# Norms of queries applied as per-partition scalars in two attentions of a two-layer encoder, and other PSUM banks for the first projections

## The chip, the core and the metric

The kernel runs on one core of a Trainium2 chip. A core has four compute engines that run at the same time, each with its own queue of instructions. TensorE (PE in the profile) multiplies matrices: it loads a stationary block of 128x128 weights (the rows "PEld") and streams the other operand past it. VectorE (DVE), ScalarE (ACT) and GpSimd (POOL) work elementwise or along rows. SyncE (SP) issues DMAs. Each works through its queue in order here, and waits on semaphores where an instruction needs what another engine has not finished. Matmul results land in PSUM, which this kernel cuts into eight banks of 128 partitions by 512 fp32 values; everything else lies in SBUF.

The metric is device time in microseconds (us). The span is the time from the first to the last instruction of one profiled execution; the time of that execution is a little longer.

## The reference, cut to what matters

The model is an encoder of two layers on 512 positions of width 1024. What the change touches is the mixer's grouped-query attention (GQA: eight query heads of width 64, two key and value heads), the attention over 256 memory tokens, and the final norm:

```python
def rms_norm(x, g):
    y = x * lax.rsqrt(jnp.mean(x * x, axis=-1, keepdims=True) + EPS)
    return y * g
...
    g_q = apply_axial_rope(rms_norm(g_q.reshape(b, s, GQA_Q_HEADS, HEAD_DIM), q_norm), cos, sin)
    g_k = apply_axial_rope(rms_norm(g_k.reshape(b, s, GQA_KV_HEADS, HEAD_DIM), k_norm), cos, sin)
...
    sc = jnp.einsum('bqkgd,bskd->bkgqs', qi, k) * scale      # GQA, one block of 128 queries
    p = jax.nn.softmax(sc, axis=-1)
    return jnp.einsum('bkgqs,bskd->bqkgd', p, v)
...
    x = x + hybrid_mixer(rms_norm(x, norm_mix[l]), ...)      # NA heads and GQA heads, then w_out
    x = x + memory_cross_attention(rms_norm(x, norm_mem_q[l]), rms_norm(mem, norm_mem_kv[l]), ...)
    x = x + conv_ffn(rms_norm(x, norm_ffn[l]), ...)
return rms_norm(x, norm_final)
```

The norm of a query head is one number per position and head. It scales a whole row of scores, so it may be applied before the scores, or in the exponential of the softmax: exp(r * s - r * max s), with r the norm of that row. The neighbourhood attention (NA) takes the other eight heads; the conv-FFN multiplies by 1024x5632 and 2816x1024.

## The kernel before, in words

**Number format and layout.** All matmuls are fp32 accurate: each operand is split in a high part (rounded, fp32r) and a low part (the rest), and most products are made as three matmuls, hi x hi, hi x lo, lo x hi (`mm3`, `gemm_T`, recorded at line 77). Activations are kept transposed: features on partitions, 512 positions along the row. Weights stream in by DMA as `raw`; ACT casts them to `hi` (L265) and POOL subtracts to get `lo` (L266); four buffers of each are in flight.

**Stages of a layer.** (1) projections of NA, in pairs of heads, and NA attention; (2) the projections of GQA; (3) GQA attention, 16 units of two heads and 128 queries; (4) the output projection's NA half, the memory's keys and values, the output projection's GQA half, closing the residual row by row (`close`, L425 to L444) into the next norm; (5) memory attention, 8 units of one head and 256 queries; (6) the FFN; (7) after the second layer the final norm and output.

**What orders the work.** PE and SP run in the order of the program text. ACT, DVE and POOL are ordered by a list scheduler of the build, in which `behind(n)` shifts an instruction's priority. The text's order comes from three helpers. `weave` runs the stages of an attention (scores, normalise, transpose, values) for staggered units. A `Filler` (`attn_fill`, `ms`) holds a list of generators, such as projections, and hands out pieces of them between the weave's steps; NA_FILL and GQA_FILL say how many. `late(n, f)` puts off a piece of work by n ticks, so that its PE instructions stand behind others while another engine prepares its operands. A moved tick moves everything that stands behind it.

**PSUM.** Three pools: `ps_mm` with four banks (projections, outputs), `ps_s` with two (scores), `ps_t` with two (transposes, sums over partitions). A bank is reused in turn; a matmul into it waits until the last reader of its former content is done.

**A GQA projection** (`gqa_project`, `gqa_rope`, L809 to L883) comes in the order k, q0, q1, v, q2, q3; each holds two heads. 48 matmuls of 128x512 fill a bank. ACT reads it twice (L840 times the gain, L841 squared) and DVE once (L842, times the cosine table). One tick later `swap` moves rows by four DMAs, and four matmuls of the squares against the constant `pairs` give the sums of squares per head and position; DVE makes the variance (L852, L855). After another tick `rotate` lets POOL take the power -1/2 (L862), copy it to whole rows (L863), and finish the rotation (L864, L865). Two ticks later `norm` turns these rows by four matmuls against the identity into a bank, L868 to L871; these are the records `mm<-ident,t`. One tick later DVE multiplies (L875) and the product is split: `split_q` (ACT copies L682, DVE subtractions L684) or `split_k` (L664, L668).

**A GQA unit** (`gqa_scores`, L888 to L904): two matmuls for each of two heads give 128x512 scores; DVE takes the negated maximum (L900), ACT the exponential with the maximum as bias and the sum accumulated (L902). `gqa_normalise` takes the reciprocal (L908) and POOL multiplies (L479). `gqa_transpose_p` follows on PE (L64), ACT (L472) and DVE (L473).

**A memory unit** (`mem_scores`, L1069 to L1084): DVE takes the negated maxima of two query blocks at once (L1076) and multiplies them by the norm `mq.rstd` (L1077), ACT takes two exponentials with that bias and the norm as scale (L1081); `normalise` (L479) is a DVE tensor_scalar whose factor is read per partition from SBUF:

```python
def normalise(e, sums, col, eng=DVE):
    eng.tensor_scalar(e, e, sums[:, col : col + 1], 1.0, op0=ALU.mult, op1=ALU.mult)
```

**The first projections** of layer 0 (`project_first`) take q0, k0 and q1 of NA interleaved as their inputs arrive, each into a bank of `ps_mm`; in layer 1 `project_qk` does the same one after the other. `split_qk` reads these banks (L650, L664 to L684). `attn_fill.step(N_FIRST ...)` (L1029) sets how many pieces run before the first scores; the pieces behind them are NA's value blocks `project_v`, each a 128x256 product in a bank of `ps_mm`.

**The final norm** (L1232 to L1253): each row is scaled by its gain `gfin` on ACT (L1241), after its square has been added up.

Of the kernel before, what the change touches and what calls it, by code (L numbers as in the profile page):

```python
# [13 lines left out]
ALU = mybir.AluOpType  # L14
# [38 lines left out]
W_BEHIND, N_RAW, N_W, AHEAD, AHEAD_HELD, N_WARM, N_LATE, N_FIRST = 45, 2, 4, 2, 5, 8, 4, 3  # L53
# [120 lines left out]
def encoder_kernel(ctx: ExitStack, tc: tile.TileContext, t: dict, out: bass.AP):  # L174
# [357 lines left out]
    mem_rep = cpool.tile([P, MEMN], F32, name="mem_rep")  # L532

# [55 lines left out]
    for l in range(DEPTH):  # L589
# [11 lines left out]
        def project_first():  # L601

            w, pms = {}, {}
            for u, k0, k1 in ((0, 0, 2), (1, 0, 2), (0, 2, 4), (1, 2, 4), (2, 0, 4), (0, 4, 6),
                              (1, 4, 6), (2, 4, 6), (0, 6, 8), (1, 6, 8), (2, 6, 8)):
                if u not in w:
                    w[u], pms[u] = get_w(NA_ORDER[u]), ps_mm()
# [23 lines left out]
        def project_qk(n, p):  # L631
            w = get_w((n, p))
            pm = ps_mm()
            gemm_T(pm, w, xg, range(0, 4), 0, KC - 1)
            yield
            gemm_T(pm, w, xg, range(4, 8), 0, KC - 1)
            if (n, p) == ("q", 0):
                mix.stat()
                held.append(pm)
            elif (n, p) == ("k", 0):  # L640
                mix.spread()
                split_qk("q", 0, held.pop())
                split_qk("k", 0, pm)
            else:
                split_qk(n, p, pm)
            yield
# [188 lines left out]
        def gqa_rope(g, pm):  # L835

            gain = qkg[:, l, 0:1] if g != "k" else qkg[:, l, 1:2]
# [6 lines left out]
            def swap():  # L844
# [3 lines left out]
                pv = ps_t()  # L848
# [9 lines left out]
            def rotate(xr, v):  # L858
                r = small(2 * NB)
                rows = tmp()  # L860
                with behind(-40):
                    POOL.tensor_tensor(r, v, mhalf[:, : 2 * NB], op=ALU.pow)  # L862
                    POOL.tensor_copy(rows.rearrange("p (b d) -> p b d", d=HD), r.unsqueeze(2).to_broadcast([P, 2 * NB, HD]))  # L863
                POOL.tensor_mul(xr, xr, gtab[0][:, 1])  # L864
                POOL.tensor_add(xr, cc, xr)  # L865
                late(2, lambda: norm(xr, rows))

            def norm(xr, rows):  # L868
# [3 lines left out]
                late(1, lambda: split(xr, pr))  # L872

            def split(xr, pr):
                DVE.tensor_mul(pr, xr, pr)  # L875
                if g == "k":
                    gk.extend(rtile((2, S)) for _ in range(2))
                    split_k(pr, gk, False)
                else:
                    gq[g] = rtile((2, S))  # L880
                    split_q(pr, gq[g])
# [6 lines left out]
        def gqa_scores(u):  # L888
# [9 lines left out]
            for j in range(2):  # L898
                c = slice(j, j + 1)
                DVE.tensor_reduce(nmx[:, c], sc[j], axis=AX.X, op=ALU.max, negate=True)  # L900
                e = tmp()
                ACT.activation(e, sc[j], AF.Exp, bias=nmx[:, c], accum_out=sums[:, c])  # L902
# [126 lines left out]
        attn_fill.step(N_FIRST if l == 0 else N_FIRST + 5)  # L1029
# [39 lines left out]
        def mem_scores(u):  # L1069
# [7 lines left out]
            DVE.tensor_mul(nmx, nmx, mq.rstd[:, 2 * bp : 2 * bp + 2])  # L1077
# [154 lines left out]
        def down_last(g):  # L1232
# [5 lines left out]
            def scale(half, m):  # L1238
                xc = xT[m][:, 256 * half : 256 * half + 256]
                with behind(20):  # L1240
                    ACT.activation(xc, xc, AF.Copy, scale=gfin[:, m : m + 1])  # L1241
# [135 lines left out]
```

## Time and profile before

| | us |
|---|---|
| runs: median of 3 (lowest, highest) | 1391.63 (1390.44, 1395.34) |
| profiled execution, its own time | 1393.77 |
| its span | 1392.0 |
| PE busy | 1354.7 |
| PE weight loads busy | 1157.8 |
| DVE busy | 834.8 |
| ACT busy | 711.8 |
| POOL busy | 719.3 |
| mean granted TensorE clock (share of full speed) | 0.994 |

The profile gives the busy time of each engine, groups of instructions by line, engine and operation (name of output <- names of inputs, partitions x elements; "x80 | 12.2, 303 | 0.0" is a count, the sum in us, the mean in ns, and the idle time ahead of them), the waits of an engine by what ended them, windows of time with the busy time of each engine, and the timeline. "L900" is line 900 of the kernel before; a line inside a helper is shared by all that call it. PE's matmuls overlap, so a group's sum on PE is more than the time it takes; differences of start times give that.

In the layers' order the stages lie at: start and NA 0 to 97 us, GQA projections 97 to 160, the rest of GQA to about 278, memory attention to 320, FFN to 704, and in layer 1 in the same order from 704 to the end, with GQA projections around 800 to 851, memory attention around 960 to 1000 and the final norm at the end.

### The profile page before, as it was taken

The numbers are of one execution on the slowest core, as the hardware profiler recorded it, in microseconds if no ns is written. First come the engines' busy times: TensorE is split into PE (matmuls) and PEld (weight loads), VectorE is DVE, ScalarE is ACT, GpSimd is POOL, SyncE is SP. The second block draws the span as 40 slices with busy tenths as digits, with TensorE's granted clock in tenths as the row PEclk, the third lists the DMA queues.
The fourth block names the chain that finished last, engine by engine and source line by source line (L and its number), as shares of the span: only waits on it lengthen the run. The fifth ranks groups of instructions, "written<-read, shape, count | busy, mean of one in ns | idle before, by whom it ended". The sixth has DMA issues, their size and how long they took to land.

```text
span 1392.0 us, 19198 instructions
## 1 busy us (share of the span) xinstructions
PE 1354.7 (97%) x7072; PEld 1157.8 (83%) x7072; DVE 834.8 (60%) x1430; ACT 711.8 (51%) x1321; POOL 719.3 (52%) x537
## 2 busy tenths in 40 slices
PE   8999899999999999999999989999999999999997
PEld 7897789877888888888888978998788888888897
DVE  6666766364787177357446556754638843871873
ACT  6676577655443134234557656766554422432453
POOL 2458776635444444444645677756264444444441
PEclk9999999999999999999999999999999999999999
DMA  7653312422333333333356523223133333333331
GB/s 214 185 145 96 87 46 66 116 63 61 98 100 103 94 91 97 101 94 94 105 147 169 139 72 95 65 71 112 40 98 97 101 91 97 98 93 106 90 93 61
DMA packets 218205, 138.83 MB, mean 100 GB/s; under 512 B 6016, under 2 KB 211072, under 8 KB 218112
## 3 DMA queue, kind: packets, MB, share of 16 engines
q1 hardware_dynamic: 217968, 137.60, 34.6%
q8 instruction: 56, 0.92, 0.3%
q14 instruction: 37, 0.30, 0.1%
q10 hardware_dynamic: 144, 0.00, 0.0%
HBM read 125.00 MB, written 2.10 MB: 91 GB/s over the span
## 4 chain that ended last, share of the span: by engine, by line
PE 89%; DVE 4%; ACT 4%; issue 1%; DMA 1%; POOL 0%; DVEq 0%; ACTq 0%; SPq 0%
PE mm L77 82%; PE sc L77 4%; PE tr L64 3%; PE tr L77 1%; ACT hi L265 1%; DVE r L473 1%; DMA raw<-in_w_in 1%; ACT t L745 1%; DVE s L900 1%; DVE s L1077 1%; DVE xg L473 0%; DVE t L842 0%; ACT t L841 0%; ACT t L840 0%; ACT xg L438 0%
## 5 line engine op out<-in xcount | busy, mean ns | idle before, releaser
L266 POOL TENSOR_TENSOR lo<-raw,hi 128x1024 fp32r<-128x1024 f32 (+2 forms) x268 | 499.0, 1874 | 496.9 <-ACT hi L265 468.9
L77 PE MATMUL mm<-xg,hi 128*128 128x512 f32 x1984 | 617.7, 393 | 3.1 <-DVE t L842 2.9
L77 PEld LDWEIGHTS mm<-xg,hi 128*128 128x128 f32 x1984 | 370.4, 189 | 78.9 <-DVE t L842 3.3
L265 ACT CAST hi<-raw 128x512 fp32r<-128x512 f32 (+2 forms) x276 | 224.6, 837 | 346.7 <-PE mm L77 292.9
L77 PE MATMUL mm<-xg,lo 128*128 128x512 f32 x992 | 387.3, 391 | 0.0
L77 PE MATMUL mm<-r,hi 128*128 128x512 f32 (+1 forms) x1144 | 331.6, 374 | 2.3 <-ACT t L444 2.2
L77 PEld LDWEIGHTS mm<-r,hi 128*128 128x128 f32 x1144 | 207.3, 188 | 39.7 <-ACT t L444 3.1
L1201 DVE SCALAR_TENSOR_TENSOR t<-t,par,t 128x7 f32<-128x7 f32 (+1 forms) x352 | 201.9, 641 | 34.0 <-ACT t L1194 34.0
L77 PEld LDWEIGHTS mm<-xg,lo 128*128 128x128 f32 x992 | 187.1, 189 | 39.6
L77 PE MATMUL mm<-r,lo 128*128 128x512 f32 (+1 forms) x572 | 213.4, 373 | 0.0
L77 PEld LDWEIGHTS mm<-r,lo 128*128 128x128 f32 x572 | 108.0, 189 | 19.0
L1186 DVE TENSOR_TENSOR t<-mm,rep 128x512 f32<-128x512 f32 x88 | 60.1, 687 | 78.2 <-PE mm L77 62.1
L479 POOL TENSOR_SCALAR t<-t,s 128x512 f32<-128x512 f32 (+1 forms) x112 | 66.3, 608 | 75.4 <-DVE s L908 35.4
L1203 ACT ACTIVATE t<-t 128x512 f32<-128x512 f32 x44 | 27.8, 633 | 134.8 <-DVE t L1201 134.7
L1207 DVE TENSOR_TENSOR r<-t,r 128x512 fp32r<-128x512 f32 x44 | 90.5, 2056 | 7.4 <-ACT r L1206 4.3
L1230 DVE TENSOR_TENSOR xT<-xT,mm 128x512 f32<-128x512 f32 x32 | 21.9, 685 | 106.8 <-PE mm L77 106.8
L64 PE MATMUL tr<-ident,t 128*128 128x128 f32 x456 | 63.2, 275 | 13.3 <-DVE r L473 3.8
L77 PE MATMUL sc<-r,r 128*128 128x256 f32 (+1 forms) x352 | 72.6, 338 | 3.5 <-DVE r L473 2.5
L64 PEld LDWEIGHTS tr<-ident,t 128*128 128x128 f32 x456 | 52.4, 141 | 22.9 <-issue 9.7
L1194 ACT ACTIVATE t<-t,par 128x512 f32<-128x512 f32 x88 | 66.8, 806 | 3.2 <-DVE t L1186 3.2
L77 PE MATMUL mm<-r,r 128*128 128x256 f32 (+1 forms) x428 | 61.8, 297 | 0.0
L77 PEld LDWEIGHTS sc<-r,r 128*128 128x128 f32 x352 | 52.1, 192 | 8.3 <-DVE r L473 3.0
(145 smaller groups left out, 1554.1 us busy)
## 6 DMA issues: line engine op xcount, KB each, us to landing
raw<-in_w_up SPq DMA_DIRECT2D x88, 512.0 KB, 3.9
raw<-in_w_in SPq DMA_DIRECT2D x33, 512.0 KB, 4.5
raw<-in_w_down SPq DMA_DIRECT2D x32, 448.0 KB, 3.9
raw<-in_w_mem_kv SPq DMA_DIRECT2D x16, 512.0 KB, 4.0
raw<-in_w_down SPq DMA_DIRECT2D x16, 512.0 KB, 4.2
r<-in_bias SPq DMA_DIRECT2D x16, 384.0 KB, 5.8
r<-r SPq DMA_DIRECT2D x22, 256.0 KB, 5.2
raw<-in_w_out SPq DMA_DIRECT2D x8, 512.0 KB, 3.8
```

What stands on the lines that cost most here:

```text
L64: return lambda *a, **k: self.tc.keep_in_program_order(op(*a, **k))
L77: return self.tc.keep_in_program_order(self.engine.matmul(out, lhsT, rhs, **k))
L265: act.copy(hi[:, k], raw[:, k])
L266: (POOL if eng[0] == "P" else DVE).tensor_sub(lo[:, k], raw[:, k], f(hi)[:, k])
L473: DVE.tensor_sub(lo, ps, f(hi))
L479: eng.tensor_scalar(e, e, sums[:, col : col + 1], 1.0, op0=ALU.mult, op1=ALU.mult)
L1186: DVE.tensor_mul(u, us[side], ffn.rep)
L1194: ACT.activation(cc, u, AF.Identity, bias=par[:, l, CB + ch : CB + ch + 1], scale=w[1])
L1201: DVE.scalar_tensor_tensor(cc[:, dst], u[:, src], wi, cc[:, dst], op0=ALU.mult, op1=ALU.add)
L1203: ACT.activation(cs[0], cs[0], AF.Silu)
L1207: DVE.tensor_sub(acts[j][1], cs[0], f(acts[j][0]))
L1230: DVE.tensor_add(xT[m], xT[m], pm)
```

## The change

For q the head norm stays a column per head and position: `rotate` writes it into one of four tiles `qr`, and `gqa_scores` multiplies the negated maximum by it with `normalise` and gives it to the exponential as its scale. The copy to rows, the four matmuls against the identity and the multiplication are left for k alone; q is split from the rotated tile `xr` in SBUF, one tick after the rotation. The sums of pairs go into a bank of `ps_mm` instead of `ps_t`. In the memory attention the product of two columns becomes two calls of `normalise`. The first two projections of each layer use the score banks. N_FIRST goes from 3 to 4 (one piece more ahead of the first scores in layer 0; in layer 1 the sum stays 8). The final gain is multiplied on DVE instead of ACT.

```diff
--- before.py
+++ after.py
@@ -50,7 +50,7 @@
 MEM_FILL = [1, 1, 2, 2, 1, 3, 1, 3, 1, 3, 1]
 N_ROWS = 3
 MEM_STEPS = [0, 0, 1, 0, 1, 1, 1, 1, 1, 1, 1] + [0] * 9
-W_BEHIND, N_RAW, N_W, AHEAD, AHEAD_HELD, N_WARM, N_LATE, N_FIRST = 45, 2, 4, 2, 5, 8, 4, 3
+W_BEHIND, N_RAW, N_W, AHEAD, AHEAD_HELD, N_WARM, N_LATE, N_FIRST = 45, 2, 4, 2, 5, 8, 4, 4
 
 
 class InOrder:
@@ -530,6 +530,7 @@
 
     mem_rstd = cpool.tile([P, MB], F32, name="mem_rstd")
     mem_rep = cpool.tile([P, MEMN], F32, name="mem_rep")
+    qr = [cpool.tile([P, 2 * NB], F32, name=f"qr{i}") for i in range(4)]
 
     def mem_stat():
         raw = load_mem()
@@ -604,7 +605,7 @@
             for u, k0, k1 in ((0, 0, 2), (1, 0, 2), (0, 2, 4), (1, 2, 4), (2, 0, 4), (0, 4, 6),
                               (1, 4, 6), (2, 4, 6), (0, 6, 8), (1, 6, 8), (2, 6, 8)):
                 if u not in w:
-                    w[u], pms[u] = get_w(NA_ORDER[u]), ps_mm()
+                    w[u], pms[u] = get_w(NA_ORDER[u]), ps_s() if u < 2 else ps_mm()
                 if (u, k0) == (0, 0):
 
                     for k in range(2):
@@ -630,7 +631,7 @@
 
         def project_qk(n, p):
             w = get_w((n, p))
-            pm = ps_mm()
+            pm = ps_mm() if p else ps_s()
             gemm_T(pm, w, xg, range(0, 4), 0, KC - 1)
             yield
             gemm_T(pm, w, xg, range(4, 8), 0, KC - 1)
@@ -834,6 +835,7 @@
 
         def gqa_rope(g, pm):
 
+
             gain = qkg[:, l, 0:1] if g != "k" else qkg[:, l, 1:2]
             xs, sq, cc = tmp(), tmp(), tmp()
             with behind(-20):
@@ -845,7 +847,7 @@
                 xr = tmp()
                 for i in range(4):
                     SP.dma_start(xr[32 * i : 32 * i + 32], xs[32 * (i ^ 1) : 32 * (i ^ 1) + 32])
-                pv = ps_t()
+                pv = ps_mm()
                 for b in range(NB):
                     PE.matmul(pv[:, 2 * b : 2 * b + 2], sq[:, b * P : (b + 1) * P], pairs, start=True, stop=True)
                 v = small(2 * NB)
@@ -856,29 +858,38 @@
                 late(1, lambda: rotate(xr, v))
 
             def rotate(xr, v):
-                r = small(2 * NB)
-                rows = tmp()
+                r = small(2 * NB) if g == "k" else qr[g]
                 with behind(-40):
                     POOL.tensor_tensor(r, v, mhalf[:, : 2 * NB], op=ALU.pow)
-                    POOL.tensor_copy(rows.rearrange("p (b d) -> p b d", d=HD), r.unsqueeze(2).to_broadcast([P, 2 * NB, HD]))
+                if g == "k":
+                    rows = tmp()
+                    with behind(-40):
+                        POOL.tensor_copy(rows.rearrange("p (b d) -> p b d", d=HD), r.unsqueeze(2).to_broadcast([P, 2 * NB, HD]))
                 POOL.tensor_mul(xr, xr, gtab[0][:, 1])
                 POOL.tensor_add(xr, cc, xr)
-                late(2, lambda: norm(xr, rows))
+                if g == "k":
+                    late(2, lambda: norm(xr, rows))
+                else:
+                    late(1, lambda: split(xr))
 
             def norm(xr, rows):
                 pr = ps_mm()
                 for b in range(NB):
                     PE.matmul(pr[:, b * P : (b + 1) * P], rows[:, b * P : (b + 1) * P], ident, start=True, stop=True)
-                late(1, lambda: split(xr, pr))
-
-            def split(xr, pr):
-                DVE.tensor_mul(pr, xr, pr)
+
+                def apply():
+                    DVE.tensor_mul(pr, xr, pr)
+                    split(pr)
+
+                late(1, apply)
+
+            def split(src):
                 if g == "k":
                     gk.extend(rtile((2, S)) for _ in range(2))
-                    split_k(pr, gk, False)
+                    split_k(src, gk, False)
                 else:
                     gq[g] = rtile((2, S))
-                    split_q(pr, gq[g])
+                    split_q(src, gq[g])
 
             late(1, swap)
 
@@ -897,9 +908,11 @@
             es = []
             for j in range(2):
                 c = slice(j, j + 1)
+                r = 2 * b + j
                 DVE.tensor_reduce(nmx[:, c], sc[j], axis=AX.X, op=ALU.max, negate=True)
+                normalise(nmx[:, c], qr[i], r)
                 e = tmp()
-                ACT.activation(e, sc[j], AF.Exp, bias=nmx[:, c], accum_out=sums[:, c])
+                ACT.activation(e, sc[j], AF.Exp, bias=nmx[:, c], scale=qr[i][:, r : r + 1], accum_out=sums[:, c])
                 es.append(e)
             ga[u] = es, sums
 
@@ -1026,7 +1039,7 @@
             out_na(), memory_keys(), memory_values(0),
             close_rows(2, PartsView(parts, 4), lambda k: whole[k], lambda: nns.append(Norm(G_MQ, l)) or nns[0],
                        memory_values(1)))
-        attn_fill.step(N_FIRST if l == 0 else N_FIRST + 5)
+        attn_fill.step(N_FIRST if l == 0 else N_FIRST + 4)
 
         def na_quanta(s):
             if s == 3:
@@ -1074,7 +1087,8 @@
                 mm3(sc[:, i, :], *(v[:, qs] for v in mqs[h]), *memk[h], True, True)
             nmx, sums = small(2), small(2)
             DVE.tensor_reduce(nmx, sc, axis=AX.X, op=ALU.max, negate=True)
-            DVE.tensor_mul(nmx, nmx, mq.rstd[:, 2 * bp : 2 * bp + 2])
+            for i in range(2):
+                normalise(nmx[:, i : i + 1], mq.rstd, 2 * bp + i)
             e = tmp((2, 256))
             for i in range(2):
                 b = 2 * bp + i
@@ -1237,8 +1251,7 @@
 
             def scale(half, m):
                 xc = xT[m][:, 256 * half : 256 * half + 256]
-                with behind(20):
-                    ACT.activation(xc, xc, AF.Copy, scale=gfin[:, m : m + 1])
+                DVE.tensor_scalar(xc, xc, gfin[:, m : m + 1], 1.0, op0=ALU.mult, op1=ALU.mult)
 
             def finish(norm):
                 norm.spread()
```

## The prediction, made before the changed kernel ran

> **What bounds the kernel now.** I read the page first (busy times, the chain that ended last), then a table of busy times by stage, then PE's waits in the stages that the change touches.
>
> ```profile
> PE 1354.7 (97%) x7072; PEld 1157.8 (83%) x7072; DVE 834.8 (60%) x1430; ACT 711.8 (51%) x1321; POOL 719.3 (52%) x537
> ...
> PE 89%; DVE 4%; ACT 4%; issue 1%; DMA 1%; POOL 0%; DVEq 0%; ACTq 0%; SPq 0%
> ```
>
> PE is busy for 1354.7 of 1392.0 us; 37 us are all that any better order can win, beside PE work taken out. Work on the other engines counts only where PE waits for it. Where PE is idle:
>
> ```profile
> 118.00:143.00 25.00, 21.66 (x128) 18.61 (x127) 15.89 (x26) 13.99 (x26) 18.34 (x17) 1.00 0.32 85
> 143.00:160.00 17.00, 15.67 (x82) 13.40 (x81) 9.85 (x20) 8.96 (x19) 13.64 (x14) 0.90 0.49 139
> ...
> 190.00:278.00 88.00, 87.03 (x561) 78.82 (x561) 50.34 (x94) 62.28 (x133) 61.19 (x58) 1.00 0.29 82
> 278.00:320.00 42.00, 39.44 (x213) 32.87 (x212) 25.13 (x57) 21.65 (x52) 10.57 (x5) 1.00 0.19 56
> 320.00:704.00 384.00, 382.88 (x1702) 317.04 (x1701) 228.56 (x318) 158.47 (x216) 185.86 (x90) 1.00 0.34 98
> ```
>
> Columns: window, its length, busy us of PE, its weight loads, VectorE (DVE), ScalarE (ACT) and GpSimd (POOL), granted clock, DMA share, GB/s. The feed-forward stretch from 320 has 1.1 us of idle PE and is not touched. The GQA projections (118 to 160) have 4.7 us and a clock below 1, the memory attention (278 to 320) has 2.6. These and the start are the places that decide.
>
> **The change part by part.** *The head norm of q.* PE loses four matmuls for each of eight q's; those for k stay.
>
> ```profile
> 116.66 1.05 PE L77 MATMUL mm<-ident,t 128*128 128x128 f32 x8
> 117.46 0.36 PE L77 MATMUL mm<-r,r 128*128 128x256 f32 x1
> ...
> L863 POOL COPY t<-s 128x512 f32<-128x512 f32 x10 | 6.1, 611 | 0.0
> ...
> L875 DVE TENSOR_TENSOR mm<-t,mm 128x512 f32<-128x512 f32 x10 | 7.0, 696 | 11.8 <-PE mm L77 10.5 <-POOL r L524 0.7 <-issue 0.7
> ```
>
> The eight records of one norm hold PE for 117.46 - 116.66 = 0.80 us. Eight q's give 6.4, and one of them stands in a half-clock stretch, so 0.8 more: -7.2 us. If half of them only stand in front of a wait, it is -3.6. POOL also loses eight copies of 0.61 and DVE eight products of 0.70, which is beside PE's work.
>
> *The first projections.* q0 and k0 take the score banks, so the v blocks find their own banks free, and one block more comes before the first scores.
>
> ```profile
> 34.84 0.35 PE L77 MATMUL mm<-hi,xg 128*128 128x256 f32 x1 [1.51 <-DVE r L684]
> ...
> 38.56 0.39 PE L77 MATMUL sc<-r,r 128*128 128x256 f32 x1 [0.27 <-DVE r L670]
> ```
>
> The block at 34.84 starts 1.51 us early, and with another block in front the scores need not wait: 1.51 + 0.27 is 1.8; the spread across block and scores (one block lasts 2.9 us, 34.84 to 37.77) leaves room for 0.4 more, so -2.2, with 0.4 to 2.5 as its ends. In layer 1 PE waits nowhere here: 0.
>
> *Memory attention.* The product of maxima and norms becomes two per-partition scalar operations.
>
> ```profile
> L1077 DVE TENSOR_TENSOR s<-s,s x16: 140/150/1917, 285.9 to 992.5; 128x2 f32<-128x2 f32 x16
> ...
> 302.64 2.38 POOL L266 TENSOR_TENSOR lo<-raw,hi 128x1024 fp32r<-128x1024 f32 x1 [7.18 <-ACT hi L265]
> 303.13 1.91 DVE L1077 TENSOR_TENSOR s<-s,s 128x2 f32<-128x2 f32 x1
> ...
> PEld sc L77 <- DVE r L473: 1.5, 1, 1.5
> PEld tr L64 <- DVE t L479: 1.2, 1, 1.2
> ```
>
> Of sixteen operations of 0.15 us some last far longer, the longest 1.91 us, while POOL's subtraction of two SBUF tensors runs; DVE is held up behind it, and in the stage the two waits of PE's weight loads above follow, 2.7 us a layer. An extra 0.15 us of DVE per unit eats 0.3 of it: 2.4 per layer, -4.7 in both. If the new form waits for POOL as well it is 0 or +0.3; if all goes, -5.4.
>
> Which it is, these rows say:
>
> ```profile
> L479 DVE TENSOR_SCALAR t<-t,s x32: 343/348/356, 288.9 to 994.5; 128x256 f32<-128x256 f32 x32
> ...
> L855 DVE TENSOR_SCALAR s<-s x10: 165/212/553, 104.1 to 836.2; 128x8 f32<-128x8 f32 x10
> ...
> L1207 DVE TENSOR_TENSOR r<-t,r x44: 680/2414/2474, 365.3 to 1347.9; 128x512 fp32r<-128x512 f32 x44
> ```
>
> The same form on 256 columns (L479, scalar by pointer) never leaves 343 to 356 ns. L855, with constants, once took 0.55. I side with L479, which has the added operation's operands. [...]
>
> *Scores of q.* Every head's maximum gains such an operation (64 of about 0.15 us) between maximum and exponentials; a unit's chain grows by 0.2 to 0.4.
>
> ```profile
> 224.09 0.30 PE L64 MATMUL tr<-ident,t 128*128 128x128 f32 x1 [0.90 <-DVE s L908]
> ```
>
> PE is busy for 87.03 of 88.00 us from 190 to 278, so in most steps the chain is covered. In a step without filler it is not: one such stall of 0.90 per layer now. The changed order has two such steps in layer 0 and one in layer 1: 0.9 + 3 x 0.3 is about +2 (1.5 to 2.5; 0 if the cover holds).
>
> *The split of q and the banks of the pairs' sums.* Losing the norm's three ticks, q is split two or three ticks earlier, from SBUF, and the order of everything behind it shifts. Now PE's weight loads wait thus between 95 and 190 (first four rows; the columns are the sum, the number and the longest), and these durations set such waits:
>
> ```profile
> PEld tr L64 <- issue: 3.1, 3, 2.1
> ...
> PEld tr L77 <- ACT t L841: 1.8, 1, 1.8
> PEld mm L77 <- DVE t L842: 1.6, 1, 1.6
> ...
> PEld tr L77 <- DVE r L473: 0.5, 1, 0.5
> ...
> L840 ACT ACTIVATE t<-mm,qkg 128x512 f32<-128x512 f32 x5 | 3.5, 693 | 0.1
> L841 ACT ACTIVATE t<-mm 128x512 f32<-128x512 f32 x5 | 3.0, 597 | 0.0
> L842 DVE SCALAR_TENSOR_TENSOR t<-mm,qkg,r 128x512 f32<-128x512 f32 x5 | 3.8, 750 | 4.3 <-ACT t L841 4.3
> ...
> L684 DVE TENSOR_TENSOR r<-mm,r 64x512 fp32r<-64x512 f32 x8 | 5.5, 689 | 1.7 <-ACT r L682 1.6
> ...
> L266 POOL TENSOR_TENSOR lo<-raw,hi 128x512 fp32r<-128x512 f32 x16 | 20.5, 1295 | 5.8 <-ACT hi L265 5.8
> L862 POOL TENSOR_TENSOR s<-s,mhalf 128x8 f32<-128x8 f32 x5 | 8.2, 1648 | 3.2 <-DVE s L855 3.1
> L864 POOL TENSOR_TENSOR t<-t,r 128x512 f32<-128x512 f32 x5 | 6.4, 1290 | 3.4 <-DVE r L473 2.7 <-DMA t<-t 0.8
> L865 POOL TENSOR_TENSOR t<-t,t 128x512 f32<-128x512 f32 x5 | 6.4, 1286 | 0.1
> L500 POOL TENSOR_TENSOR r<-t,r 128x512 fp32r<-128x512 f32 x3 | 3.8, 1281 | 2.3 <-PE mm L77 1.6 <-ACT r L499 0.7
> ```
>
> Layer 0 loses 2.1 + 1.8 + 1.6 + 0.5 = 6.0 us in the GQA projections, and layer 1, whose stretch from 800 to 851 has 6.3 us of idle PE (first row of the next fence), about as much. Followed through the changed order, PE meets in layer 0:
> - q1's projection, which waits for the bank of q0's (0.69 + 0.60 on ACT, then 0.75 on DVE, behind one weight cast): 2.5;
> - q2's projection, now whole in one piece, which waits for v's bank, whose reader is queued behind q0's two subtractions (2 x 0.69): 0.7 to 4, taken as 2;
> - q3's pairs straight behind its projection, so both ACT reads bare and their hand-overs, with weight casts between: 2.4;
> - the NA output's first rows, in one piece, which need the last NA pair's low part (L500). On POOL it stands behind a weight split, two rotations and a power: 1.30 + 2 x (1.29 + 1.29) + 1.65 + 1.28 = 9.4, begun 1.3 (both ACT reads) after the projection's end; PE's own work up to there is about 6.8: 3.9.
>
> Sum 10.8 (9.5 to 14.6). Layer 1, in the same way: 3.4 for q0's bank behind two transposes, 2.3 for q1's, 3.0 for the third transpose, and 4.0 for q3's pairs, whose bank is read only after six other DVE operations: 12.5 (10.5 to 15). Beside 6.0 each that is +11.3 (+8 to +17.6). If the orders are looser than that, 0.
>
> *Clock.* Such stalls can cost twice:
>
> ```profile
> 800.00:851.00 51.00, 44.65 (x242) 38.12 (x240) 30.34 (x54) 30.30 (x66) 40.87 (x45) 0.93 0.34 98
> ...
> 150.80:154.00 3.20, 3.20 (x13) 2.87 (x12) 0.32 (x1) 0.00 (x0) 3.20 (x5) 0.51 0.71 191
> ...
> 148.91 0.27 PE L77 MATMUL tr<-pairs,t 128*128 128x2 f32 x1 [1.33 <-ACT t L841]
> ...
> 138.67 0.30 PE L64 MATMUL tr<-ident,t 128*128 128x128 f32 x1 [1.91 <-DVE r L473]
> ```
>
> Soon after the 1.33 at 148.91 PE ran 3.2 us at half clock, which costs 1.6; the 1.91 at 138.67, in the stretch 118 to 143 with its clock of 1.00, was followed by none. I add one such stretch: +1.6 (0 to +4.8). [...]
>
> *Final scale.* Sixteen ACT operations become DVE's.
>
> ```profile
> 1383.70 0.16 DVE L400 TENSOR_SCALAR s<-tr 128x2 f32<-128x2 f32 x1 [1.37 <-PE tr L77]
> ```
>
> The last one, 0.35 us on DVE (L479's row), fits into DVE's 1.37 us of idleness before L400: 0; if it comes later, +0.35.
>
> **Sum.** -7.2 - 2.2 - 4.7 + 2 + 11.3 + 1.6 = +0.8 us. The profiled execution took 1393.77, its span and 1.8 around it, and stands 2.1 above the runs' median of 1391.63; so 1394.6 for such an execution, 1392.4 for the median.
>
> **The rivals.** *A: the stalls at the GQA start don't grow.* For it: freed banks and 0.70 + 0.61 us less DVE and POOL work for each q; against it the queues above. The terms left are -14.1 + 2 = -12.1, with 0 to +4 of new waits: 1379.5 to 1384, about 1381.
> *B: slower, by the subtractions of q's split.* They now have two SBUF inputs, while POOL is busy for 18.34 of 25 us at 118 to 143. L1207 shows that pair at 2.41 instead of 0.69. A collision adds 0.6 (half of a weight split of 1.30) to a DVE queue on which PE waits. Sixteen of them at 0.6 are 9.6; it decides from seven on (4.2 us): about 1402.
> *C: 128x1 operations wait for POOL as L855 once did.* The memory term is 0 instead of -4.7, and the GQA chains lose some 2 more: +7.5, 1399. L479 speaks against it.
> *D: the edit takes matmuls out only ahead of waits*, so that -7.2 is -3.6: +4.4, 1396.
>
> **How the numbers follow.** About 0.3%, 4.2 us, is what a measurement of this kernel can tell from no change. My forecast (1386 to 1398) 0.38, of which 0.12 faster, 0.20 same, 0.06 slower; A 0.27, faster; B 0.18, slower; C 0.09, slower; D 0.08, half same, half slower. That is faster 0.39, same 0.24, slower 0.37. The range reaches from A's end to B's and 2 beyond, 1379 to 1404; the forecast's own is 1386 to 1398.
>
> **What would show it.** mm<-ident,t at 16 records where there are 80; no wait for L684's successor near 34.8; the two memory waits gone and no 128x1 operation above 0.3 us; q's subtractions at 0.69 or longer beside POOL; PE idle for about 10 us between 118 and 160, 4.7 now. The prediction is wrong if that idle time is not larger, if those subtractions are longer than 1.3 us, or if the clock falls more than twice per layer.

## The result: 0.7% slower

The changed kernel takes 1402.71 us (median of 5 runs, 1400.41 to 1404.04) where the kernel before, in its 5 runs, takes 1392.13 (1390.44 to 1395.34): a ratio of 1.0067 with a 95% interval of 1.0047 to 1.0087, or +9.3 us. The profiled execution took 1403.0 us, its span is 1401.2, 9.2 longer than before. Below, a run's difference in us is what its ratio has above or below 1, times 1392.

The page of the changed kernel, its busy times and its chain:

```profile
PE 1355.3 (97%) x7008; PEld 1152.0 (82%) x7008; DVE 845.5 (60%) x1518; ACT 707.8 (51%) x1305; POOL 719.5 (51%) x529
...
PE 85%; DVE 5%; ACT 4%; POOL 2%; DMA 2%; issue 1%; SPq 0%; DVEq 0%; ACTq 0%; POOLq 0%
```

PE has 64 records less, but is busy for 0.6 us more, and idle for 1401.2 - 1355.3 = 45.9 us where it was 37.3. So 8.6 of the 9.2 us are waits. That PE's busy time did not fall by the 6.4 us of the matmuls agrees with the clock: its mean is 0.989 where it was 0.994. What full speed would have saved is 0.011 x 1401 = 15.4 us now and 0.006 x 1392 = 8.4 before, so some 7 us more are lost to reduced speed (about 1 either way, by the rounding of the clock).

The windows of the GQA projections, the GQA attention and the memory attention, and three short stretches (columns as in the prediction's tables):

```profile
118.00:160.00 42.00, 36.38 (x183) 30.25 (x181) 28.98 (x48) 26.70 (x53) 35.71 (x35) 0.92 0.37 102
...
190.00:280.00 90.00, 85.19 (x540) 75.33 (x539) 52.02 (x110) 62.68 (x132) 57.81 (x54) 0.98 0.25 71
282.00:327.00 45.00, 44.66 (x237) 37.13 (x236) 27.34 (x71) 24.79 (x57) 12.72 (x6) 1.00 0.16 48
140.20:143.60 3.40, 3.40 (x18) 3.21 (x18) 2.23 (x5) 1.26 (x3) 3.40 (x4) 0.59 0.40 101
150.80:154.10 3.30, 3.30 (x9) 2.58 (x9) 2.58 (x4) 3.25 (x6) 2.31 (x3) 0.53 0.00 1
256.60:260.00 3.40, 3.40 (x10) 2.60 (x9) 2.05 (x3) 1.53 (x2) 1.97 (x2) 0.54 0.56 167
```

The memory attention lost its idle time (0.3 of 45 us; 2.6 of 42 before). The projections have 5.6 us instead of 4.7, and the GQA attention, which had 1.0 of 88, has 4.8 of 90. From 118 us on, layer 0 has the three slow stretches of the last rows, where before had one. The same stages of layer 1, before and then after:

```profile
800.00:851.00 51.00, 44.65 (x242) 38.12 (x240) 30.34 (x54) 30.30 (x66) 40.87 (x45) 0.93 0.34 98
851.00:966.00 115.00, 114.03 (x715) 102.20 (x714) 65.95 (x122) 79.86 (x173) 77.74 (x77) 1.00 0.26 74
...
802.00:855.00 53.00, 44.34 (x218) 36.26 (x217) 29.87 (x57) 31.68 (x66) 41.17 (x39) 0.90 0.33 97
855.00:975.00 120.00, 114.28 (x703) 99.90 (x702) 67.59 (x147) 79.92 (x170) 77.97 (x79) 1.00 0.24 70
```

There the projections are idle for 8.7 us instead of 6.3, and what follows them, which had 1.0, for 5.7. So in both layers the idle time grew more behind the projections than in them. The timeline of PE names the waits, in layer 0 and then in layer 1:

```profile
139.88 1.07 PE L77 MATMUL mm<-pairs,t 128*128 128x2 f32 x8 [2.07 <-ACT t L843]
...
148.79 0.50 PE L77 MATMUL mm<-r,hi 128*128 128x512 f32 x1 [2.26 <-ACT r L499]
...
150.58 0.50 PE L77 MATMUL mm<-r,hi 128*128 128x512 f32 x1 [1.29 <-POOL r L500]
...
183.47 0.63 PE L64 MATMUL tr<-ident,t 128*128 128x128 f32 x4 [2.91 <-POOL t L479]
...
256.14 0.50 PE L77 MATMUL mm<-r,hi 128*128 128x512 f32 x1 [1.95 <-POOL r L492]
...
825.13 1.08 PE L64 MATMUL tr<-ident,t 128*128 128x128 f32 x4 [4.08 <-DVE r L473]
...
839.02 1.05 PE L77 MATMUL mm<-pairs,t 128*128 128x2 f32 x8 [2.62 <-ACT t L843]
...
944.25 0.50 PE L77 MATMUL mm<-r,hi 128*128 128x512 f32 x1 [1.95 <-POOL r L492]
```

The first three are the pairs of q3 and the NA output's rows; the prediction had these, and in layer 1 the transposes at 825 and the pairs at 839. It did not have the other three: transposes that wait for POOL at 183, and the output projection that waits for the last folded halves (L492) at 256, and the same at 944 in layer 1. Taking the same instruction in both traces as a landmark: the first scores of NA stand 0.5 us later, with a block of 2.9 us more done; the first memory scores of layer 0 4.4 us later (284.17 to 288.56), the last 2.3 later; the last wait for the closing of layer 1's memory attention 6.9 later (1008.61 to 1015.53), and the end 9.2. So each layer loses about 7 us between its first scores and its memory attention, and gets 2.1 back there.

The durations of what was added, by line:

```profile
L479 DVE TENSOR_SCALAR s<-s,qr x64: 194/204/216, 149.4 to 923.2; 128x1 f32<-128x1 f32 x64
L479 DVE TENSOR_SCALAR s<-s,s x32: 201/204/216, 290.3 to 1000.3; 128x1 f32<-128x1 f32 x32
...
L685 DVE TENSOR_TENSOR r<-t,r x16: 684/687/1724, 122.9 to 847.6; 64x512 fp32r<-64x512 f32 x16
...
L915 ACT ACTIVATE t<-sc,s,qr 128x512 f32<-128x512 f32 x64 | 49.4, 777 | 32.9 <-DVE s L479 32.8
...
L1254 DVE TENSOR_SCALAR xT<-xT,gfin x16: 340/347/2001, 1358.5 to 1391.5; 128x256 f32<-128x256 f32 x16
```

None of the 96 operations of 128x1 is over 0.216 us, though 37 of them began while POOL worked on two tensors; q's subtractions reach 1.72, and the exponentials went from 0.693 to 0.777.

### The profile page after: what moved, and what is told of

Read it like the earlier page. It is cut to its first block, busy times and chain, and to the rows that moved or that the text cites. A ratio compares the mean times of both kernels' runs of the same rounds, so it can differ in the third digit from the quotient of the medians.

```text
span 1401.2 us, 19111 instructions
## 1 busy us (share of the span) xinstructions
PE 1355.3 (97%) x7008; PEld 1152.0 (82%) x7008; DVE 845.5 (60%) x1518; ACT 707.8 (51%) x1305; POOL 719.5 (51%) x529
## 4 chain that ended last, share of the span: by engine, by line
PE 85%; DVE 5%; ACT 4%; POOL 2%; DMA 2%; issue 1%; SPq 0%; DVEq 0%; ACTq 0%; POOLq 0%
PE mm L77 77%; PE sc L77 4%; PE tr L64 3%; DMA raw<-in_w_in 1%; ACT hi L265 1%; DVE s L912 1%; PE tr L77 1%; POOL lo L266 1%; DVE xg L473 1%; ACT t L915 1%; SPq L64 0%; POOL t L479 0%; DMA raw<-in_w_down 0%; DMA r<-in_memT 0%; DVE t L455 0%
## 5 line engine op out<-in xcount | busy, mean ns | idle before, releaser
L77 PE MATMUL mm<-xg,hi 128*128 128x512 f32 x1920 | 596.0, 392 | 1.4 <-DVE t L844 1.4
L77 PEld LDWEIGHTS mm<-xg,hi 128*128 128x128 f32 x1920 | 357.9, 189 | 73.5 <-DVE t L844 1.6
L77 PE MATMUL mm<-xg,lo 128*128 128x512 f32 x960 | 374.5, 390 | 0.0
L77 PE MATMUL mm<-r,hi 128*128 128x512 f32 (+1 forms) x1144 | 335.6, 377 | 10.0 <-POOL r L492 3.9
L77 PEld LDWEIGHTS mm<-xg,lo 128*128 128x128 f32 x960 | 180.6, 188 | 38.2
L479 POOL TENSOR_SCALAR t<-t,s 128x512 f32<-128x512 f32 (+1 forms) x112 | 66.2, 607 | 77.7 <-DVE s L921 35.2
L915 ACT ACTIVATE t<-sc,s,qr 128x512 f32<-128x512 f32 x64 | 49.4, 777 | 32.9 <-DVE s L479 32.8
```

The source lines that it names most:

```text
L77: return self.tc.keep_in_program_order(self.engine.matmul(out, lhsT, rhs, **k))
L915: ACT.activation(e, sc[j], AF.Exp, bias=nmx[:, c], scale=qr[i][:, r : r + 1], accum_out=sums[:, c])
```

## The experiments

**One part at a time.** Four kernels carry one part of the change each, on the kernel before.

```diff
# mem_only
-            DVE.tensor_mul(nmx, nmx, mq.rstd[:, 2 * bp : 2 * bp + 2])
+            for i in range(2):
+                normalise(nmx[:, i : i + 1], mq.rstd, 2 * bp + i)
# banks_only: the three lines of project_first, project_qk and N_FIRST (and N_FIRST + 4)
# pairs_only
-                pv = ps_t()
+                pv = ps_mm()
# qnorm_only: rotate, norm, split and gqa_scores as changed, all else as before
```

> Kernel before with only the memory attention's product of maxima and norms as two per-partition scalar operations. Theory 1 (each part acts in its own stage, and the traces of before and after show it there): memory attention shorter by 2.1 us in each layer, nothing elsewhere, so 4.2 us faster (ratio 0.997); the 1.5 us waits of the weight loads of the memory's scores are gone and no 128x1 operation is over 0.3 us. Rival (the stage is bound by PE and the gain in the changed kernel came from what ran before it): below 1.5 us.

> Kernel before with only the first two projections of a layer in the score banks, and one value block more ahead of the first scores in layer 0. Theory 1: 2 to 2.5 us faster, all in layer 0 before 110 us: the wait of 1.51 us at the second value block and of 0.27 at the scores go. Rival (the block that is taken earlier is missing as filler later on): 0 to 1 us faster, with a new wait between 90 and 190 us.

> Kernel before with only the sums of pairs in the projections' banks. Theory 1: within 3 us of before, since the waits for the transposes' banks ahead of the pairs (0.5 us a layer) go and the ring of four banks has one user more. Rival (the projections' banks are scarce): slower by 4 to 12 us, with new waits of projections and outputs for a bank between 97 and 190 and between 800 and 860 us.

> Kernel before with only q's head norm as the exponentials' scale (maxima multiplied, q split from SBUF one tick after the rotation); sums of pairs stay in the transposes' banks. Theory 1 (the loss of the whole change is q's norm, by the order of the work that shifts): slower by 8 to 16 us although PE loses 6.4 us of matmuls. Rival (the sums of pairs in the projections' banks are what costs): faster by 0 to 6 us.

| kernel | ratio to before (95%) | us |
|---|---|---|
| mem_only | 0.9973 (0.9963 to 0.9983) | -3.8 |
| banks_only | 0.9990 (0.9981 to 0.9999) | -1.4 |
| pairs_only | 1.0000 (0.9991 to 1.0008) | 0 |
| qnorm_only | 1.0180 (1.0166 to 1.0194) | +25.1 |

Memory is as theory 1 has it. In its window from 270 to 320 PE's weight loads waited thus before: 1.5 (scores), 1.2 (transposes), 0.9 and 0.4; with the new form, in the same window:

```profile
PEld tr L64 <- issue: 1.1, 2, 0.7
PEld tr L64 <- DVE t L479: 0.5, 1, 0.5
PEld mm L77 <- DVE r L473: 0.2, 1, 0.2
```

The banks are worth less than the stalls that they remove. In the profiled execution PE is idle for 1390.2 - 1355.6 = 34.6 us instead of 37.3, which is theory 1's size, but it is busy for 0.9 us longer, at a mean clock of 0.992 instead of 0.994. Between 90 and 190, where the rival looked for its wait, there is only one of 0.55 us, at 147.26. But with the block taken earlier a longer one comes further on:

```profile
251.34 0.80 PE L77 MATMUL mm<-r,hi 128*128 128x512 f32 x1 [1.95 <-POOL r L492]
```

Before does not wait here. It has 1.4 us of other products (from 249.01) behind the last units' values, which now stand ahead of them, and POOL makes the folded half ahead of its weight splits, where it now stands behind two of them, 2.51 us in all. A slow stretch goes with the wait: the matmul behind it takes 0.80 us, where that at 256.14 in the changed kernel takes 0.50. So the rival's cause is there, beside theory 1's, and the wait at 256 in layer 0 of the changed kernel comes with the banks alone. In layer 1, where the number of pieces ahead of the scores stays 8, banks_only has no such wait. Also, in each of its runs the time is 2.2 us over the span, where it is 1.8 in before's: 0.4 of the gain is lost outside the span, which no run explains. The pairs' bank does nothing alone. q's norm costs more than the whole change does, although it takes matmuls out. Its waits are those of the changed kernel and longer ones; three of the longest in layer 0, from PE's timeline:

```profile
138.94 0.63 PE L64 MATMUL tr<-ident,t 128*128 128x128 f32 x4 [4.09 <-DVE r L473]
...
152.02 1.05 PE L77 MATMUL tr<-pairs,t 128*128 128x2 f32 x8 [2.62 <-ACT t L843]
...
261.56 0.50 PE L77 MATMUL mm<-r,hi 128*128 128x512 f32 x1 [1.95 <-POOL r L492]
```

**Why q's norm costs.** The `Filler` subtracts from what it owes the modelled time of every matmul that is issued in a step, whoever issues it. Without the norm's matmuls (NB, which is 4, at 107 ns each: 428 ns for each q) it hands out pieces earlier, and PE's whole order behind the first q changes. Three kernels separate this from the work itself. The first is q's norm with the missing time still counted and q split at its old tick, so that PE's order is that of before less 32 matmuls; the other two keep PE's order and add one piece of q's new work each.

```diff
# qnorm_counted, against qnorm_only
-                    late(1, lambda: split(xr))
+                    def count():
+                        PE.ns += NB * 107.0
+                        late(1, lambda: split(xr))
+
+                    late(2, count)
# sbuf_split, against before: for q, split from SBUF
+                if g != "k":
+                    DVE.tensor_mul(xr, xr, pr)
+                    pr = xr
+                else:
+                    DVE.tensor_mul(pr, xr, pr)
# max_ops, against before (one_col is a column of ones)
+                normalise(nmx[:, c], one_col, 0)
-                ACT.activation(e, sc[j], AF.Exp, bias=nmx[:, c], accum_out=sums[:, c])
+                ACT.activation(e, sc[j], AF.Exp, bias=nmx[:, c], scale=one_col, accum_out=sums[:, c])
```

> q's head norm as the exponentials' scale, alone as in the run with q's norm only, but the four matmuls that go are still counted (428 ns) when the filler hands out pieces, and q is split at its old tick: PE's order is that of before with 32 matmuls left out. Theory 2 (the 25 us that q's norm cost alone come from the filler: it counts the modelled time of every matmul, so that without the norm's it hands out pieces in another order, and projections come straight behind the work that they wait for): all but 5 us of the 25 go, 1384 to 1396. Rival 2a (the subtractions from SBUF and the longer way from maximum to exponential cost it): it stays at 1408 or more.

> Kernel before, with q's product with its norm written to SBUF instead of PSUM, and q split from there: PE's order is that of before, DVE's sixteen subtractions have two SBUF inputs. Theory 2: under 4 us slower; sixteen subtractions of 0.69 to 1.7 us each, 0.26 us more on average as in the changed kernel's trace, partly beside PE's work. Rival 2a: 8 us or more.

> Kernel before, with every maximum of the grouped-query attention multiplied by a column of ones in a per-partition scalar operation, and that column as the exponential's scale: PE's order is that of before, 64 operations of 0.20 us more on DVE and exponentials of 0.78 instead of 0.69 us. Theory 2: 1 to 4 us slower, in the steps without filler. Rival 2a: 8 us or more.

| kernel | ratio to before (95%) | us |
|---|---|---|
| qnorm_counted | 1.0068 (1.0056 to 1.0081) | +9.5 |
| sbuf_split | 1.0022 (1.0012 to 1.0031) | +3.1 |
| max_ops | 1.0039 (1.0025 to 1.0053) | +5.4 |

The counted time takes 15.6 of the 25.1 us away, so on the kernel before the order is the larger part; but it leaves 9.5, more than theory 2 had, and less than its rival. The two kinds of work, 3.1 and 5.4, were both above or near the upper end of what was expected of them. They add up to 8.5. If they add up in the kernel as well, which no run shows, the 32 matmuls changed the time by about +1 instead of -6.4.

Since PE's order is the same but for the norms, the traces of before and qnorm_counted can be laid side by side, instruction by instruction. The eight norms do go, and save 8.3 us where they stood (0.81 to 0.89 each, and 1.56 for the two in slow stretches). The gain is lost at other places. PE's timeline of qnorm_counted:

```profile
137.16 0.63 PE L64 MATMUL tr<-ident,t 128*128 128x128 f32 x4 [2.86 <-DVE r L473]
...
150.22 1.05 PE L77 MATMUL tr<-pairs,t 128*128 128x2 f32 x8 [2.61 <-ACT t L843]
...
174.66 0.58 PE L77 MATMUL tr<-ones,t 128*128 128x1 f32 x4 [2.77 <-DVE s L479]
```

Before, the first two waits were 1.91 (at 138.67) and 1.33 (at 148.91), and there was none at the third. In front of the first, and of these three only there, stood a norm that covered a part of it:

```profile
135.27 1.06 PE L77 MATMUL mm<-ident,t 128*128 128x128 f32 x8
136.17 0.60 PE L64 MATMUL tr<-ident,t 128*128 128x128 f32 x4
```

It held PE for 0.89 us, and the wait is 0.95 longer without it; the same in layer 1, so 1.9 us of the gain were cover. The second wait is 1.28 longer in layer 0 and 1.64 in layer 1 (2.97 for 1.33), and no norm stood in front of it. There it is ACT: a q that needs no norm from PE is ready for its split earlier, and the split's casts now run ahead of the squares on which the pairs wait:

```profile
146.55 1.26 ACT L683 CAST r<-t 64x512 fp32r<-64x512 f32 x2
...
149.58 0.59 ACT L843 ACTIVATE t<-mm 128x512 f32<-128x512 f32 x1
```

In before ACT goes from its cast at 146.00 straight to the weights' casts, and the squares begin at 148.27. The third wait is DVE's order, in layer 0 alone: the ones multiply a sum of the memory's squares (L543), which DVE makes at 174.10, behind two maxima, where before has it at 172.32, ahead of them:

```profile
174.10 0.41 DVE L543 TENSOR_TENSOR t<-t 128x256 f32<-128x256 f32 x1
```

These are readings of the traces; no run holds the casts or that sum back alone. The clock adds to them: qnorm_counted runs at half speed for five times 3.4 us ahead of the last stage, before for three (a clock of 0.50 from 150.84, 823.27 and 836.92 on); the means are 0.992 and 0.994.

In max_ops no new wait is over 0.9 us; the units follow each other more slowly. The 16 units' first scores stand at 146.51 and their last at 230.10 before, at 147.31 and 233.03 in max_ops: 2.1 us more in layer 0. The largest steps are scores that wait for an exponential (0.8 to 0.9 us where before does not wait, twice in layer 0 and once in layer 1). DVE's line there shows the operations themselves, and who waits:

```profile
L479 DVE TENSOR_SCALAR s<-s,one_col x64: 198/204/216, 149.2 to 923.1; 128x1 f32<-128x1 f32 x64
...
  ACT t L905: 32.5, 28
  PE tr L64: 5.0, 8
```

In sbuf_split the sixteen subtractions from SBUF take 1.19 us on average, those from PSUM 0.69:

```profile
L684 DVE TENSOR_TENSOR r<-t,r 64x512 fp32r<-64x512 f32 x16 | 19.0, 1185 | 1.8 <-ACT r L682 1.4
L684 DVE TENSOR_TENSOR r<-mm,r 64x512 fp32r<-64x512 f32 x16 | 11.0, 689 | 3.0 <-ACT r L682 2.7
```

**The order alone.** The opposite test: nothing is changed but the account. All instructions of before are there; the norm's time is subtracted again, so that PE's order is that of qnorm_only with the 32 matmuls in it.

```diff
# order_only, in norm(), against before
+                if g != "k":
+                    PE.ns -= NB * 107.0
```

> Kernel before with every instruction kept, but the four matmuls of q's norm are not counted when the filler hands out pieces: PE's order is that of the run with q's norm only, plus the 32 matmuls. Theory 2 (the filler's account shifts the order, and the order costs): slower by 10 to 18 us, the difference between the uncounted and the counted run of q's norm being 16, with waits of 2 us and more for the transposes in the projections and a wait for the folded halves (POOL r) near 256 and 944. Rival 2b (the order costs only together with the earlier, longer work of q's norm): under 5 us slower.

It is slower by a ratio of 1.0092 (1.0074 to 1.0111), 12.8 us. An account of 428 ns in eight places, with no change in any engine's work, costs as much as the whole change does, or more. Three of its longest waits in layer 0:

```profile
165.44 1.23 PE L64 MATMUL tr<-ident,t 128*128 128x128 f32 x8 [2.39 <-DVE xg L473]
...
174.11 0.68 PE L64 MATMUL tr<-ident,t 128*128 128x128 f32 x4 [3.34 <-DVE s L910]
...
259.87 0.79 PE L77 MATMUL mm<-r,hi 128*128 128x512 f32 x1 [1.94 <-POOL r L492]
```

The last one is the wait for L492 that before has nowhere, and its cause is as in banks_only: the 1.4 us of products have been handed out ahead of the last values, and POOL takes two weight splits ahead of the fold. It comes in layer 1 as well, at 948.75 (1.94 us), as in the changed kernel at 944; the uncounted order alone brings it there. The first two are at transposes of the GQA attention, near places where before waits 1.68 and 0.67 us.

**The final gain.** Where the last feed-forward ends, the changed kernel falls back by another 1.8 us (at 1340 us of before PE's instructions stand 6.9 us later, at 1360 8.7), and one gain operation there took 2.00 us.

```diff
# final_only
-                with behind(20):
-                    ACT.activation(xc, xc, AF.Copy, scale=gfin[:, m : m + 1])
+                DVE.tensor_scalar(xc, xc, gfin[:, m : m + 1], 1.0, op0=ALU.mult, op1=ALU.mult)
```

> Kernel before with only the final gain on DVE. The traces of before and after differ by 1.8 us behind the last feed-forward, with one gain operation of 2.00 us beside a weight split of POOL. Theory 3 (the gain on DVE collides with POOL's split of the last weights and delays it): 1 to 3 us slower, with a wait of PE near 1357 us. Rival (the 1.8 us came from the order of the weights' transfers, which the earlier stages shifted): within 0.7 us of before.

The ratio is 0.9998 (0.9989 to 1.0007): nothing, and theory 3 falls. One gain operation takes 2.00 us here as well, and PE does not wait. What delayed the changed kernel's execution there is a wait of 1.54 us at 1366.52 for the split of the last weights, whose cast on ACT had waited for their transfer. qnorm_counted, with the gain on ACT as before, has the same wait (1.34 us at 1365.43). So it is not the gain; why the transfer came later stays open.

**Parts together.** Three kernels ask whether the parts add up.

```diff
# after_counted: the changed kernel, with the count() of qnorm_counted
# after_pairst: the changed kernel, with
-                pv = ps_mm()
+                pv = ps_t()
# mem_banks: the edits of mem_only and banks_only on the kernel before
```

> The changed kernel with the four matmuls of q's norm still counted by the filler, and q split at its old tick. Theory 2 with parts that add up (q's norm counted +9.5, memory -3.9, first banks -1.3, final gain 0, pairs' banks 0): 4 us above before, 1396 to 1398, and 6 below the changed kernel. Rival (with the pairs in the projections' banks the uncounted order costs little): 1400 to 1404, like the changed kernel.

> The changed kernel with the sums of pairs back in the transposes' banks. q's norm alone (there the sums stood in those banks) cost 25 us, the whole change 10.6 though memory and first banks give back 5.2: some 10 us are unexplained. Theory 4 (in the uncounted order the pairs stand right among transposes and wait for their two banks; alone, in the order of before, moving them was worth 0): 1408 to 1414. Rival (the first banks and the block taken earlier have shifted the filler back to a better order): 1400 to 1405, like the changed kernel.

> Kernel before with only the memory attention's scalar operations and the first projections' banks. The sum of the two alone is -3.9 - 1.3 = -5.2 us: 1386 to 1388 if they add up, faster than both kernels. Rival (they meet in the same waits, or the shifted half-clock stretches take it back): 1388 to 1391.

| kernel | ratio to before (95%) | us |
|---|---|---|
| after_counted | 1.0022 (1.0012 to 1.0032) | +3.1 |
| after_pairst | 1.0068 (1.0056 to 1.0080) | +9.5 |
| mem_banks | 0.9963 (0.9950 to 0.9975) | -5.2 |

With the time counted the parts do add up: 9.5 - 3.8 - 1.4 = 4.3 was to be expected, 3.1 is measured. The uncounted order then costs 9.3 - 3.1 = 6.2 in the changed kernel, where it cost 15.6 on the kernel before. In layer 1 the wait for L492 is gone with the time counted; in layer 0 it stays (1.95 us at 253.98), since the banks bring it. Theory 4 on that difference falls: with the pairs back in the transposes' banks the kernel is no slower. The block of values that is taken earlier shifts what the filler has left, and PE's order in layer 0 differs from that of qnorm_only from there on; that this is the cause was argued, no run separates it. The version that leaves q's norm alone, mem_banks, is 5.2 us faster than before (median 1387.38) and has the lowest time of those run, though its interval overlaps that of mem_only.

## Why the prediction was right, and where it was not

The time lies in the range (1379 to 1404), near its upper end, and outside the forecast's own (1386 to 1398); the point of 1392.4 was 10 us too low, and the case that came true is the slower side, to which the text gave 0.37. The wide range held because rival B's end was in it, and B's sixteen collisions are not what carried the time: that is luck more than mechanism. Of the three signs by which the text would be wrong, two came: three of q's sixteen subtractions took longer than 1.3 us (1.66, 1.67 and 1.72), and in layer 0 the clock fell three times from 118 us on and once ahead of that. PE's idle time at 118 to 160 did grow, but by 0.9 us and not by five. By its steps:

- **Memory attention, -4.7:** measured -3.8 (-5.2 to -2.4). Right in size, and the two waits went as said: no 128x1 operation waits for POOL. Rival C is refuted by 96 operations of 0.194 to 0.216 us, of which 37 began beside a POOL operation on two tensors. But the row that decided it, L479's, was no test: of its 32 operations of 128x256 only two met a subtraction of POOL, and for its last 0.19 us. The same form at 128x256 took 2.00 us in the one case that began inside a subtraction (last section). To side with that row was right by luck.
- **First projections, -2.2:** the two stalls went as said; alone the part is worth -1.4 (-2.6 to -0.1). The term left out what the block would be missed for: the wait of 1.95 us for the fold, at 251 in banks_only and 256 in the changed kernel.
- **Final gain, 0:** measured -0.3 (-1.5 to +1.0). Right.
- **Pairs' banks:** they were counted among the shifted waits; alone they are 0, and in the changed kernel too.
- **Head norm of q, -7.2:** right for the matmuls themselves: the records fell from 80 to 16, and 8.3 us went where they stood. But with the order kept little or nothing of it is left. 1.9 us stood ahead of a wait, as rival D had it (it allowed for 3.6 and had 0.08); 2.9 us more went to the pairs' waits behind the split's casts on ACT and as much to a sum on DVE, for which the text had no term.
- **Scores of q, +2:** mis-sized, +5.4 (3.5 to 7.4). The price of one operation, 0.15, was a tensor_tensor's; this form takes 0.20. The exponential's longer time with a scale by pointer (0.08 us for each of 64) was left out, and cover was taken for whole steps where a step has slack in one place only.
- **Split from SBUF:** it had no term of its own in the sum and only a place in rival B, which gave sixteen collisions 9.6 us. They cost 3.1 (1.7 to 4.3): B's mechanism, a third of its size.
- **Stalls at the GQA start, +11.3:** wrong in size and in place; the idle time of the two projection stages grew by 0.9 and 2.3 us. Single waits were well seen: q3's pairs were 2.4 and measured 2.07; the NA output's rows 3.9, measured 2.26 + 1.29 = 3.55. q1's 2.5 and q2's 2 did not come in layer 0. In layer 1, 3.0 for a transpose became 4.08, 4.0 for the pairs 2.62, and 3.4 and 2.3 became 1.37 and none. What was not seen is what the order does further on: 2.91 at 183 and 1.95 at 944, beyond the windows that were followed (and 1.95 at 256, which the banks bring too). Behind the projections PE's idle time grew by 3.8 us in layer 0 (190 to 280) and by 4.7 in layer 1. PE's idle time at 118 to 160 is 5.6 us, not about 10. (Layer 1's four stalls add up to 12.7 and not 12.5, on which nothing hangs.)
- **Clock, +1.6:** mis-sized; the mean clocks give about 7. Layer 0 alone has two slow stretches more, 3.41 us at a clock of 0.50 each, behind stalls of 2.07 and 1.95 us (139.88 and 256.14), and one from 7.67 us on, which max_ops, with before's first 30 us, has too (two matmuls of 128x512 take 1.06 us there at 10.89, and 0.64 at 12.17). In layer 1 one lasts twice as long, 6.8 us from 823.45.

The errors partly cancel: the stalls at the GQA start and what is left of the matmuls' gain were both taken too large, the work on maxima and the clock too small. What the text lacked is the filler's account, 6.2 us of the changed kernel's 9.3 and 15.6 of the 25.1 that q's norm costs alone: it followed the order that resulted, but priced it as eight separate waits, and did not ask how PE's order would stand if the matmuls had been counted. The other part, q's norm with the order kept, is 9.5 us alone and more than pays for what memory and banks give back.

Rival A is refuted by its total, since it allowed for at most 4 us of new waits and PE is idle for 8.6 us more; but in its own place, the GQA start, the stalls grew by only some 3. The point where B decides, seven collisions of 0.6 us, was not reached in time: all sixteen subtractions together cost 3.1.

## What to carry to other kernels

Where a program's order is made by counting the modelled time of what is issued, taking an instruction out moves everything behind it: keep the account first, measure, and re-tune the order after that. Matmuls that stand in front of a wait are cover and not cost; look at what the next instruction waits for before counting them as a gain. And where they were what held back another engine's work, ask ahead of what that work will now run. A row decides between two theories only if its operations met the case in question: count those that did. A product of two small columns on VectorE that sits on a chain beside GpSimd's two-input work is worth making a per-partition scalar operation, which no such work delayed here at 128x1 (0.216 us at most; -3.8 us for the kernel).

## What the runs showed of the hardware that was not expected

The same form of operation took no longer beside POOL's work at one width, and once far longer at another. All 96 of 128x1 took 0.194 to 0.216 us, and 35 of them lay wholly inside a POOL operation on two tensors. The thirty-two of 128x256 in the memory attention took 0.343 to 0.355, but hardly met such work: two of them, for 0.19 us. The one that began inside a subtraction, the first gain on 128x256, took 2.00 us, here and in the three other kernels with the gain on DVE (final_only, after_counted, after_pairst); the other fifteen gains of the changed kernel took 0.340 to 0.354. On the timelines of the two engines:

```profile
1358.25 2.12 POOL L266 TENSOR_TENSOR r<-raw,r 128x896 fp32r<-128x896 f32 x1 [0.37 <-ACT r L265]
1358.52 2.00 DVE L1254 TENSOR_SCALAR xT<-xT,gfin 128x256 f32<-128x256 f32 x1 [1.24 <-ACT t L444]
```

It ended 0.15 us behind the subtraction. In before the 128x2 products of two tensors (L1077) are alike: four of sixteen began inside a POOL subtraction and took 1.47 to 1.92 us, the other twelve 0.14 to 0.15. Of q's subtractions those from SBUF took 1.72 us at most, those from PSUM 0.69. Why a column of one element took no longer there, and the gain did, no run shows.

The clock was 0.50 behind some of PE's waits, for 3.41 us at a time in layer 0. In the trace of the changed kernel the three stretches above begin at 140.79, 151.03 and 256.84; the waits ahead of them are 2.07 us, 2.26 with 1.29 behind it, and 1.95. Not every such wait had one: a wait of 1.91 us was followed by a slow stretch in max_ops (at 137.91; two matmuls of 128x512 take 1.05 us there at 140.81, and 0.63 at 142.02) and in layer 1 of before (at 823.15; 0.50 from 823.27 on), and by none in layer 0 of before (at 138.67), where the shorter one of 1.33 at 148.91 was followed by one from 150.84 on. What decides it no run shows. In kernels with the same matmuls the profiled executions' mean clock went from 0.992 to 0.996 (mem_only 0.994, banks_only 0.992, final_only 0.996), some 5 us of time at full speed, which is as much as most of the parts above.
